# Attention scores with the low part of the keys on half of the array's rows, and an order of work without a table of corrections

## The chip, the cores and the metric

One core of one Trainium2 chip runs the whole program. The metric is the device time of one execution in microseconds (us). A run's time differs from another's of the same kernel by less than 0.2%: three runs of the kernel before took 614.14, 614.48 and 614.99 us.

## The reference, cut to what matters

Two layers, each on 256 positions of 1024 channels. One layer projects the normalised input to the operands of three causal attention mixers (a, b, c), of 8 heads of 64 channels each, and of an indexer with 8 query heads and one key head, gates each mixer's output, projects and merges the three, and adds the result to the residual.

```python
h = rms_norm(x, gain)
proj = jnp.einsum('bsd,de->bse', h, w_in)               # 9808 columns
# mixers a, b, c: per head, over the causal keys (b: over the 64 keys that the indexer picks)
s = jnp.einsum('bhqd,bhkd->bhqk', q, k) * scale         # + a forget bias in c
p = jax.nn.softmax(jnp.where(mask, s, -jnp.inf))
o = jnp.einsum('bhqk,bhkd->bhqd', p, v)
# indexer: 8 query heads, one key head
rel = jax.nn.relu(jnp.einsum('bqhd,bsd->bqhs', q_idx, k_idx))
isc = jnp.einsum('bqh,bqhs->bqs', w_idx, rel)
y = jnp.einsum('nbsw,nwd->bsnd', jnp.stack([oa, ob, oc]) , w_branch)
out = x + jnp.einsum('bsd,de->bse', jnp.sum(gates * y, axis=2), w_out)
```

## The kernel before

**Precision.** Every operand of a matmul is split into a high part (the value rounded to the type that TensorE reads in one pass) and a low part (value minus high part). A product of two operands is the sum of three products: high by high, low by high, high by low. For a weight the split is an ACT copy (`hi`, L401) and a DVE subtraction (`lo`, L405) of a 128x1024 piece; six pieces can be ready at a time (the rings `wh` and `wl`).

**Projections.** `unit_b` (L458) computes 128 output channels for all 256 positions with 24 matmuls of 256 columns, all from line 446 (`mm_ops`); `unit_a` (L475) computes 512 channels of V or of the output with matmuls of 512 columns. Three PSUM banks `proj` take turns.

**Scores.** Two heads make a pair: a projection unit gives their 64 + 64 channels on the 128 partitions. `write_q` (L611) makes three tiles: `qh`, the high part of both heads; `qx`, the high part of the first head over its low part; `qy`, the low part of the second head over its high part. `write_bd` (L766) makes the keys: `bd..h` holds two groups of 256 columns, and in group h the high part of head h stands on both halves of the partitions (one ACT copy of both heads into both groups, then one half copied across in each group, L782); `bd..l` also holds two groups of 256 columns, the low part of head 0 on the upper 64 partitions of group 0, the low part of head 1 on the lower 64 partitions of group 1, and zeros elsewhere. The zeros are written once at the start (L970 to L978). The two low parts are two DVE subtractions of 64 partitions (L784). `scores` (L626) then does, for each of two blocks of 128 queries (128 keys for the first, 256 for the second), one matmul with `qh` as the weights and both groups of `bd..l` as the moving operand (L635: 256 and 512 columns; the zeros keep the heads apart) and one matmul for each head with `qx` or `qy` as the weights and that head's `bd..h` group moving (L637: 128 or 256 columns), which adds high by high and low by high in one go, since the two stand on different rows. So bank `s0` holds the first query block of both heads, bank `s1` the second. There are 16 such groups of six matmuls in a layer (12 pairs of the mixers, 4 of the indexer), 32 in all.

**After the scores.** For a mixer's pair, DVE adds the bias and finds the extreme of each row (L696), ACT takes the exponential (L700), the normalised rows are transposed on TensorE (L723), split again (L726, L728) and multiplied with V (L739 to L742). For the indexer ACT takes the relu of the two banks (L851, L852) and DVE sums the heads (L860, L862).

**The order of the work.** The code doesn't issue instructions as it goes. It records operations, each with its engine, its cost by a formula, what it reads and writes, and a key (about the number of the projection unit to which it belongs, minus or plus a lead). `Plan.run` (L170) then places them one at a time: on the engine that can start something first, of the operations that can start then it takes the one with the lowest key. PSUM banks and buffers are handed out in that same order. What comes out is a fixed order on each engine; on the chip each engine works its list off in order and waits at semaphores. A table, `SHIFT` (L75), gives some 240 of the operations, by their number, a correction of their key (from -9 to +2).

One place in this kernel already uses a part of the array's rows: the transposes of `wf` (L798), which hold the indexer's weights and the forget logits. They read 16 partitions from partition 64 on, and the built program gives them a tile of 32 rows by 128 columns at row 64. The two matmuls at L741 and L742 use a tile of 128 rows by 64 columns at the origin. All the others use the whole array.

Of the kernel before, what the change touches and what calls it, by code (L numbers as in the profile page):

```python
# [9 lines left out]
F32 = mybir.dt.float32  # L10
# [42 lines left out]
def shape_constants():  # L53
# [18 lines left out]
    return c  # L72


SHIFT = {  # L75
# [21 lines left out]
}  # L97


CUR = [""]  # L100
PLAN_T = [0]
PREV = {}
# [19 lines left out]
class Plan:  # L122
# [8 lines left out]
    def op(self, ways, reads, writes, key, lag=0.0, name="", touch=()):  # L131
# [18 lines left out]
                o.bufs.append(t)  # L150
        o.deps = list(deps.values())
        o.n, o.out, o.need, o.end = len(self.ops), [], 0, None
        o.key += SHIFT.get(o.n, 0.0)
        for d in o.deps:
            if d is not o:
                d.out.append(o)
# [114 lines left out]
def hybrid_trunk(ctx, tc, x, norm_gain, w_in, forget_bias, w_branch, w_out, final_gain, consts, out):  # L271
# [49 lines left out]
    hTl = pool.tile([128, KC, S], F32R, name="hTl")  # L321
    og = [[pool.tile([128, 4, S], F32R, name=f"og{i}{p}") for p in "hl"] for i in range(2)]
    NBD = 3
    bd = [[pool.tile([128, 2, S], F32R, name=f"bd{i}{p}") for p in "hl"] for i in range(NBD)]
    pts = [pool.tile([128, 2, 384], F32R, name=f"pt{p}") for p in "hl"]

    cst = pool.tile([128, C_END], F32, name="cst")
# [19 lines left out]
    ncs = pool.tile([128, 2, 8], F32, name="ncs")  # L347
    widx = pool.tile([128, 2, 8], F32, name="widx")

    k_id, k_rope, k_gT, k_bdz, k_cst, k_fb, k_wf, k_widx, k_lf, k_cs = (Tok() for _ in range(10))  # L350
    k_cT, k_row = Tok(), [Tok() for _ in range(6)]
    k_isc = [Tok() for _ in range(2)]
    k_selb = [Tok() for _ in range(2)]
# [272 lines left out]
    def scores(q, k, ktoks, key, margin=MARGIN, shared=False):  # L626
        s0, s1 = Buf("s"), Buf("s")
        kt = [t for h in ktoks for t in h]
        q, kx = q

        def go():
            qh, x = T(q[0]), [T(q[1]), T(q[2])]
            kh, kl = T(k)
            for o, sl, n in ((T(s0)[:, :256], slice(0, 128), 128), (T(s1), slice(128, 256), 256)):
                PE.matmul(o.rearrange("p (h c) -> p h c", h=2), qh[:, sl], kl[:, :, :n], start=True, stop=False)  # L635
                for h in range(2):
                    PE.matmul(o[:, h * n:(h + 1) * n], x[h][:, sl], kh[:, 0 if shared else h, :n], start=False, stop=h == 1)  # L637
        pe(go, 811.0, [q[0], q[1], q[2], k] + kx + kt, [s0, s1], key, "qk", margin)
        return s0, s1

    class Pair:
# [44 lines left out]
        def attend(self, key):  # L686
# [3 lines left out]
            for h in range(2):  # L690
                b, bt, bb = bs[h]
                e, st = Buf("e"), Buf("st")
                kt = [Tok(), Tok()]
                parts = ((0, 0, 128, s0), (1, 128, 256, s1))
                for t, a, n, s in parts:
                    dve(lambda t=t, a=a, n=n, s=s, e=e, st=st, b=b, h=h: DVE.tensor_tensor_reduce(  # L696
                        T(e)[:, a:a + n], T(s)[:, h * n:(h + 1) * n], b(a, n), 1.0, 3e38, ALU.add, ALU.min,
                        T(st)[:, t:t + 1]), n, [s, bt[t]], [kt[t]], key, "max", touch=[e, st] + bb)
                for t, a, n, s in parts:
                    act(lambda t=t, a=a, n=n, e=e, st=st: ACT.activation(  # L700
# [65 lines left out]
    def write_bd(src, b, toks, key, ps, shared=False):  # L766

        up, dn = slice(0, 64), slice(64, 128)
        if not shared:
            act(lambda: ACT.activation(T(b)[0], T(src)[:, :S].unsqueeze(1).to_broadcast([128, 2, S]), AF.Copy), 2 * S, ps, [src],  # L770
                [toks[0][0], toks[0][1], toks[1][0], toks[1][1]], key, "bd", touch=[b])
        else:
            act(lambda: ACT.activation(T(b)[0][up, 0], T(src)[up, :S], AF.Copy), S, ps, [src], [toks[0][0]], key, "bd", touch=[b],
                half=True)
        for h, o in enumerate((up, dn)):
            g, x = (0, up) if shared else (h, o)
            s = lambda x=x: T(src)[x, :S]
            hi = lambda x=x, g=g: T(b)[0][x, g]
            lo = lambda o=o, h=h: T(b)[1][o, h]
            if not (shared and h):  # L780
                y = dn if x is up else up
                act(lambda hi=hi, y=y, g=g: ACT.activation(T(b)[0][y, g], hi().bitcast(F32), AF.Copy), S, False, [toks[g][0]],  # L782
                    [toks[g][1]], key, "bd", touch=[b], half=True)
            dve(lambda hi=hi, lo=lo, s=s: DVE.tensor_tensor(lo(), s(), hi().bitcast(F32), op=ALU.subtract), S,  # L784
                [src, k_bdz, toks[g][0]], [toks[h][2]], key, "bd", touch=[b], port=not ps, half=True)

    def ev_kwf(l, ps, key):
        act(lambda: ACT.activation(wf[64:80], T(ps)[64:80, :S], AF.Copy), S, True, [ps], [k_wf, k_cT], key, "wf")
# [56 lines left out]
    def index_scores(p, ps, kb, ktoks, key):  # L845
        r = rope(ps, key)
        q = write_q((lambda: T(r), r), False, key, name="qi")
        s0, s1 = scores(q, kb, ktoks, key + 1, QK_MARGIN, True)
        base = (p % 2) * 768
        rel = [tmp6[:, base:base + 256], tmp6[:, base + 256:base + 768]]  # L850
        act(lambda: ACT.activation(rel[0], T(s0)[:, :256], AF.Relu), 256, True, [s0], [k_tmp[p % 2]], key + 1, "relu")  # L851
        act(lambda: ACT.activation(rel[1], T(s1), AF.Relu), 512, True, [s1], [k_tmp[p % 2]], key + 1, "relu")  # L852
        for h in range(2):
            hd = 2 * p + h
            for t, (a, n) in enumerate(((0, 128), (128, 256))):
                rr = rel[t][:, h * n:(h + 1) * n]
                w = widx[:, t, hd:hd + 1]
                o = isc[:, a:a + n]
                if hd == 0:
                    f = lambda rr=rr, w=w, o=o: DVE.tensor_scalar(o, rr, w, None, op0=ALU.mult)  # L860
                else:
                    f = lambda rr=rr, w=w, o=o: DVE.scalar_tensor_tensor(o, rr, w, o, op0=ALU.mult, op1=ALU.add)  # L862
                dve(f, n, [k_tmp[p % 2], k_widx], [k_isc[t]], key + 1, "isc", t_dve(n) + 61.0, port=True)
# [103 lines left out]
        load(fbias.rearrange("p l h -> p (l h)"),  # L967
             forget_bias.rearrange("(o l) h -> o (l h)", o=1).to_broadcast([128, L * 8]), 8192, [k_fb], -12 + 2.6, "fb")
    late_loads()
    dve(lambda: DVE.memset(isc, 0.0), 384, [], [k_isc[0], k_isc[1]], 0.5, "zero")  # L970
    for b in bd:
        for t in b[1:]:
            z = t.rearrange("p h c -> p (h c)")
            plan.op([(e, c, lambda z=z, f=f, a=a: f(z[:, a:a + 256], isc[:, :256]))
                     for e, c, f in (("DVE", t_dve2(256), DVE.tensor_copy),) for a in (0,)],
                    [k_isc[0], k_isc[1]], [k_bdz], 1.0, 0.0, "zero")
            dve(lambda z=z: DVE.tensor_copy(z[:, 256:], isc[:, :256]), 256, [k_isc[0], k_isc[1]], [k_bdz], 1.0, "zero",
                t_dve2(256))  # L978

    hA = (lambda k, t: hTh[:, k, t * 128:(t + 1) * 128], lambda k, t: hTl[:, k, t * 128:(t + 1) * 128])  # L980
    mA = (lambda k, t: merged(k)[0][:, t * 128:(t + 1) * 128], lambda k, t: merged(k)[1][:, t * 128:(t + 1) * 128])
# [168 lines left out]
```

## Time and profile before

| what | value |
|---|---|
| median of 3 runs | 614.48 us |
| the profiled execution's own time | 614.35 us |
| its span, first to last instruction | 612.5 us |
| mean granted TensorE clock | 0.997 |
| TensorE (PE), matmuls | 4804 |
| DVE busy, of the span | 88% |
| ACT busy, of the span | 71% |
| what moved from HBM | 103.37 MB, 170 GB/s over the span |

A row of the timeline gives the start in us from the span's start, the duration in us, the engine, the line, the operation, what it writes and reads, its shapes (weights' rows*columns, then partitions x columns that move) and how many it merges. PE is a matmul and PEld the load of its weights, which the profile shows as instructions of their own. Matmuls follow one another in a pipeline: a duration of 0.28 us covers the way through the array as well, and what a matmul costs in a row of them is the distance from its start to the next one's.

### The profile page before, as it was taken

To read this page: it belongs to the slowest core of one execution; us is meant where nothing else is said; L and a number is where in the kernel's file an instruction comes from. 1 tells how busy PE (TensorE), PEld (TensorE's weight loads), DVE (VectorE), ACT (ScalarE), POOL (GpSimd) and SP (SyncE) were. 2 spreads that over 40 slices of the span, in tenths; PEclk is the share of its full clock that TensorE was granted. 3 is DMA by queue.
4 is the path that set the end of the run, shared out by engine and by line. 5 is a ranking of instruction groups with operands and counts; after the bars stand their busy time and mean duration, and the time that the engine had idled before them with its cause. 6 is when DMAs were issued, how large, how long until landed. Compare 5 with 4: busy or idle time off the path is not lost.

```text
span 612.5 us, 12615 instructions
## 1 busy us (share of the span) xinstructions
PE 603.7 (99%) x4804; PEld 580.1 (95%) x4804; DVE 536.5 (88%) x1332; ACT 437.1 (71%) x913; POOL 92.3 (15%) x98
## 2 busy tenths in 40 slices
PE   8999999999999999999999999999999999999995
PEld 6999999899998999999889999999999989999985
DVE  8899999986998899989588999999689978999873
ACT  5687597686985678875587766968689756976641
POOL 1242331000000335000006205100000014220001
PEclk9999999999999999999999999999999999999998
DMA  9963847556354655276455639284538356445411
GB/s 295 349 201 102 258 138 226 171 175 203 131 182 138 201 175 171 76 256 213 138 176 182 193 108 288 77 258 159 178 104 279 101 174 204 139 139 182 162 36 68
DMA packets 96156, 107.32 MB, mean 175 GB/s; under 512 B 4576, under 2 KB 84832, under 8 KB 96096
## 3 DMA queue, kind: packets, MB, share of 16 engines
q1 hardware_dynamic: 95808, 106.13, 54.6%
q8 instruction: 37, 0.61, 0.4%
q10 hardware_dynamic: 288, 0.39, 0.2%
q14 instruction: 23, 0.19, 0.1%
HBM read 103.37 MB, written 1.05 MB: 170 GB/s over the span
## 4 chain that ended last, share of the span: by engine, by line
PE 96%; DVE 1%; issue 1%; DMA 0%; POOL 0%; ACT 0%; POOLq 0%; DVEq 0%
PE proj L446 84%; PE t L723 3%; PE s L637 2%; PE s L635 2%; PE proj L1029 1%; PE o L742 1%; PE o L739 1%; DMA x<-in_x_dram 0%; PE o L741 0%; PE o L740 0%; DVE wl L1021 0%; DVE hTl L561 0%; DVE wh L1019 0%; PE t L547 0%; DVE tmp L513 0%
## 5 line engine op out<-in xcount | busy, mean ns | idle before, releaser
L446 PE MATMUL proj<-hTh,wh 128*128 128x256 f32 (+1 forms) x1040 | 270.3, 278 | 0.0
L446 PE MATMUL proj<-hTl,wh 128*128 128x256 f32 (+1 forms) x1040 | 270.0, 277 | 0.0
L405 DVE TENSOR_TENSOR wl<-raw,wh 128x1024 fp32r<-128x1024 f32 (+1 forms) x190 | 231.6, 1228 | 30.7 <-ACT wh L401 29.3
L446 PE MATMUL proj<-hTh,wl 128*128 128x256 f32 (+1 forms) x1040 | 234.0, 278 | 0.0
L401 ACT ACTIVATE wh<-raw 128x1024 fp32r<-128x1024 f32 (+1 forms) x190 | 199.9, 1055 | 46.9 <-PE proj L446 44.0
L446 PEld LDWEIGHTS proj<-hTh,wh 128*128 128x128 f32 (+1 forms) x1040 | 194.7, 187 | 0.3
L446 PEld LDWEIGHTS proj<-hTl,wh 128*128 128x128 f32 (+1 forms) x1040 | 194.7, 187 | 0.3
L446 PEld LDWEIGHTS proj<-hTh,wl 128*128 128x128 f32 (+1 forms) x1040 | 175.7, 187 | 0.0
L496 POOL TENSOR_TENSOR rsh<-rsh,cst 128x256 f32<-128x256 f32 (+1 forms) x42 | 35.1, 837 | 346.5 <-DVE rsh L495 346.2
L700 ACT ACTIVATE e<-e,st 128x128 f32<-128x128 f32 (+1 forms) x96 | 42.8, 449 | 12.2 <-DVE st L696 11.7
L498 POOL TENSOR_TENSOR rr<-rr,rsh 128x256 f32<-128x256 f32 (+1 forms) x42 | 50.9, 1211 | 3.6 <-DVE rr L497 0.3
L446 PE MATMUL proj<-wh,v 128*128 128x512 f32 (+1 forms) x144 | 35.5, 368 | 0.0
L446 PE MATMUL proj<-og0l,wh 128*128 128x256 f32 x128 | 33.8, 276 | 0.0
L446 PE MATMUL proj<-og0h,wh 128*128 128x256 f32 x128 | 32.3, 277 | 0.0
L446 PE MATMUL proj<-wh,hTh 128*128 128x512 f32 x80 | 32.1, 401 | 0.0
L446 PE MATMUL proj<-wh,hTl 128*128 128x512 f32 x80 | 31.3, 392 | 0.0
L446 PEld LDWEIGHTS proj<-wh,v 128*128 128x128 f32 x144 | 25.2, 188 | 4.7
L446 PE MATMUL proj<-og0h,wl 128*128 128x256 f32 x128 | 28.6, 276 | 0.0
L728 DVE TENSOR_TENSOR ptl<-t,pth 128x384 fp32r<-128x384 f32 x48 | 25.0, 550 | 1.1 <-ACT pth L726 0.9
L446 PE MATMUL proj<-wl,hTh 128*128 128x512 f32 x80 | 24.9, 392 | 0.0
L899 ACT ACTIVATE mth<-proj 128x256 f32<-128x256 f32 x32 | 12.2, 381 | 16.9 <-PE proj L446 16.8
L446 PEld LDWEIGHTS proj<-og0h,wh 128*128 128x128 f32 x128 | 24.0, 188 | 0.0
(195 smaller groups left out, 1048.4 us busy)
## 6 DMA issues: line engine op xcount, KB each, us to landing
raw<-in_w_in_dram SPq DMA_DIRECT2D x74, 1024.0 KB, 5.3
raw<-in_w_branch_dram SPq DMA_DIRECT2D x24, 512.0 KB, 3.7
raw<-in_w_out_dram SPq DMA_DIRECT2D x8, 1024.0 KB, 6.2
tmp<-wf SPq DMA_DIRECT2D x16, 128.0 KB, 5.6
raw<-in_w_in_dram SPq DMA_DIRECT2D x3, 512.0 KB, 6.6
x<-in_x_dram SPq DMA_DIRECT2D x4, 256.0 KB, 4.3
raw<-in_w_in_dram SPq DMA_DIRECT2D x2, 320.0 KB, 5.7
out_dram<-tmp SPq DMA_DIRECT2D x2, 320.0 KB, 2.4
```

The source lines that it names most:

```text
L401: ACT.activation(p[0].v, sel(c.v), AF.Copy)
L405: DVE.tensor_tensor(p[1].v, sel(c.v), p[0].v.bitcast(F32), op=ALU.subtract)
L446: PE.matmul(o(), a(), b(), start=first and i == 0, stop=last and i == n - 1)
L496: gps(lambda: POOL.tensor_tensor(T(sh)[:np_], T(sh)[:np_], s[:np_], op=ALU.mult), S, [k_rope], [sh], key, "rope")
L498: gps(lambda: POOL.tensor_tensor(T(r)[:np_], T(r)[:np_], T(sh)[:np_], op=ALU.add), S, [sh], [r], key, "rope")
L635: PE.matmul(o.rearrange("p (h c) -> p h c", h=2), qh[:, sl], kl[:, :, :n], start=True, stop=False)
L637: PE.matmul(o[:, h * n:(h + 1) * n], x[h][:, sl], kh[:, 0 if shared else h, :n], start=False, stop=h == 1)
L700: act(lambda t=t, a=a, n=n, e=e, st=st: ACT.activation(T(e)[:, a:a + n], T(e)[:, a:a + n], AF.Exp, bias=T(st)[:, t:t + 1], scale=-1.0, acc ...
L723: PE.transpose(T(ps)[:, i * 128:(i + 1) * 128], T(es[h])[:, i * 128:(i + 1) * 128], ident)
L728: dve(lambda h=h, src=src: DVE.tensor_tensor(T(pl)[:, h], src(), T(ph)[:, h].bitcast(F32), op=ALU.subtract), 384, [ps, kp[h][0]], [kp[h][1 ...
L739: PE.matmul(ov, v[:, 0, hd], T(ph)[:, h, a], start=h == 0, stop=False)
L899: act(lambda: ACT.activation(T(th), T(ps)[:, :S], AF.Tanh, scale=0.5), S, True, [ps], [th], u - EARLY, "mth")
```

## The change

- `bd..l` becomes one tile of 256 columns: the low part of head 0 on partitions 0 to 63, that of head 1 on partitions 64 to 127. There are no zeros in it, and the zeroing at the start goes. For a pair it is written by one DVE subtraction of 128 partitions, which reads group 0 of `bd..h` before head 0's high part is copied across over the lower half; that copy (ACT) now waits for the subtraction. For the indexer's single key head there are still two subtractions of 64 partitions.
- `scores` does the products with low keys as matmuls of 64 rows, one per head: head 0 with tile position (0, 0), head 1 with (64, 0). Four of them come first (both heads on 128 columns, both heads on 256), then the four with `qx` and `qy` on all 128 rows: eight matmuls for six. The moving columns are 128 + 128 + 256 + 256 in the first four, where there were 256 + 512.
- Bank `s0` now holds head 0 and bank `s1` head 1, 384 columns each. What reads the banks follows: the relu reads 384 columns of each bank where it read 256 and 512.
- The group's cost in the planner is 700 where it was 811.
- The table `SHIFT` and its use go, so that every operation's key is the one that the code gives it, and the planner's order changes on all engines.

```diff
-SHIFT = {
-    115: 1, 142: -6.5, 144: -0.5, 145: -7, 146: -1, 148: -3, 150: -5, 160: 2, 172: 2, 173: -6, 174: -1, 192: -4,
...
-        o.key += SHIFT.get(o.n, 0.0)
...
-    bd = [[pool.tile([128, 2, S], F32R, name=f"bd{i}{p}") for p in "hl"] for i in range(NBD)]
+    bd = [[pool.tile([128, 2, S], F32R, name=f"bd{i}h"), pool.tile([128, S], F32R, name=f"bd{i}l")] for i in range(NBD)]
...
-            for o, sl, n in ((T(s0)[:, :256], slice(0, 128), 128), (T(s1), slice(128, 256), 256)):
-                PE.matmul(o.rearrange("p (h c) -> p h c", h=2), qh[:, sl], kl[:, :, :n], start=True, stop=False)
+            o = [T(s0), T(s1)]
+            cols = ((slice(0, 128), 0, 128), (slice(128, 256), 128, 256))
+            for sl, a, n in cols:
                 for h in range(2):
-                    PE.matmul(o[:, h * n:(h + 1) * n], x[h][:, sl], kh[:, 0 if shared else h, :n], start=False, stop=h == 1)
-        pe(go, 811.0, [q[0], q[1], q[2], k] + kx + kt, [s0, s1], key, "qk", margin)
+                    r = slice(64 * h, 64 * h + 64)
+                    PE.matmul(o[h][:, a:a + n], qh[r, sl], kl[r, :n], start=a == 0, stop=False, tile_position=(64 * h, 0),
+                              skip_group_check=True)
+            for sl, a, n in cols:
+                for h in range(2):
+                    PE.matmul(o[h][:, a:a + n], x[h][:, sl], kh[:, 0 if shared else h, :n], start=False, stop=a > 0,
+                              skip_group_check=True)
+        pe(go, 700.0, [q[0], q[1], q[2], k] + kx + kt, [s0, s1], key, "qk", margin)
...
+        def across(y, x, g):
+            act(lambda: ACT.activation(T(b)[0][y, g], T(b)[0][x, g].bitcast(F32), AF.Copy), S, False, [toks[g][0]],
+                [toks[g][1]], key, "bd", touch=[b], half=True)
+
         if not shared:
             act(lambda: ACT.activation(T(b)[0], T(src)[:, :S].unsqueeze(1).to_broadcast([128, 2, S]), AF.Copy), 2 * S, ps, [src],
                 [toks[0][0], toks[0][1], toks[1][0], toks[1][1]], key, "bd", touch=[b])
...
+            across(up, dn, 1)
+            dve(lambda: DVE.tensor_tensor(T(b)[1], T(src)[:, :S], T(b)[0][:, 0].bitcast(F32), op=ALU.subtract), S,
+                [src, toks[0][0], toks[0][1]], [toks[0][2], toks[1][2]], key, "bd", touch=[b], port=not ps)
+            across(dn, up, 0)
+            return
...
-        act(lambda: ACT.activation(rel[0], T(s0)[:, :256], AF.Relu), 256, True, [s0], [k_tmp[p % 2]], key + 1, "relu")
-        act(lambda: ACT.activation(rel[1], T(s1), AF.Relu), 512, True, [s1], [k_tmp[p % 2]], key + 1, "relu")
+        for h, sh in enumerate((s0, s1)):
+            act(lambda h=h, sh=sh: ACT.activation(rel[h], T(sh)[:, :384], AF.Relu), 384, True, [sh], [k_tmp[p % 2]], key + 1, "relu")
...
-    dve(lambda: DVE.memset(isc, 0.0), 384, [], [k_isc[0], k_isc[1]], 0.5, "zero")
-    for b in bd:
```

PE's list, at the first group of the indexer's scores (`qh` to `qy` are the query tiles, `s` the score banks, `proj` a projection's bank), before:

```order
L446 MATMUL proj_166<-hTl,wh_67 128x256
L635 MATMUL s_167<-bd0l,qh_80 128x256
L637 MATMUL s_167<-bd0h,qx_83 128x128
L637 MATMUL s_167<-bd0h,qy_86 128x128
L635 MATMUL s_168<-bd0l,qh_80 128x512
L637 MATMUL s_168<-bd0h,qx_83 128x256
L637 MATMUL s_168<-bd0h,qy_86 128x256
L446 MATMUL proj_166<-hTh,wl_74 128x256
```

and the same place of PE's list with the change:

```order
L420 MATMUL proj_166<-hTl,wh_67 128x256
L613 MATMUL s_167<-bd0l,qh_80 128x128
L613 MATMUL s_168<-bd0l,qh_80 128x128
L613 MATMUL s_167<-bd0l,qh_80 128x256
L613 MATMUL s_168<-bd0l,qh_80 128x256
L617 MATMUL s_167<-bd0h,qx_83 128x128
L617 MATMUL s_168<-bd0h,qy_86 128x128
L617 MATMUL s_167<-bd0h,qx_83 128x256
L617 MATMUL s_168<-bd0h,qy_86 128x256
L420 MATMUL proj_166<-hTh,wl_74 128x256
```

Here nothing has moved but the group itself: the two rows with `bd0l` have become four, all ahead of the `bd0h` rows.

The third score group of mixer a in the first layer, before, on PE (it stands inside a V unit of 512-column matmuls):

```order
L446 MATMUL proj_166<-wl_74,hTh 128x512 x2
L635 MATMUL s_168<-bd0l,qh_80 128x256
L637 MATMUL s_168<-bd0h,qx_83 128x128
L637 MATMUL s_168<-bd0h,qy_86 128x128
L635 MATMUL s_167<-bd0l,qh_80 128x512
L637 MATMUL s_167<-bd0h,qx_83 128x256
L637 MATMUL s_167<-bd0h,qy_86 128x256
L446 MATMUL proj_166<-wh_68,hTh 128x512
```

and with the change (it stands inside a unit of 256-column matmuls):

```order
L420 MATMUL proj_166<-hTl,wh_67 128x256
L613 MATMUL s_167<-bd0l,qh_80 128x128
L613 MATMUL s_168<-bd0l,qh_80 128x128
L613 MATMUL s_167<-bd0l,qh_80 128x256
L613 MATMUL s_168<-bd0l,qh_80 128x256
L617 MATMUL s_167<-bd0h,qx_83 128x128
L617 MATMUL s_168<-bd0h,qy_86 128x128
L617 MATMUL s_167<-bd0h,qx_83 128x256
L617 MATMUL s_168<-bd0h,qy_86 128x256
L420 MATMUL proj_166<-hTh,wh_67 128x256
```

This group has moved up by 120 projection matmuls (756 of them stand ahead of it before, 636 now), and its fourth neighbour by 108. Of the 32 groups, 15 have moved, 10 of them up and 5 down.

More of the change, by code (lines that the diff above doesn't have):

```diff
@@ L72, in shape_constants @@
     return c
-SHIFT = {
[21 rows of a table removed]
-}
 CUR = [""]
@@ L348, in hybrid_trunk @@
     widx = pool.tile([128, 2, 8], F32, name="widx")
-    k_id, k_rope, k_gT, k_bdz, k_cst, k_fb, k_wf, k_widx, k_lf, k_cs = (Tok() for _ in range(10))
+    k_id, k_rope, k_gT, k_cst, k_fb, k_wf, k_widx, k_lf, k_cs = (Tok() for _ in range(9))
     k_cT, k_row = Tok(), [Tok() for _ in range(6)]
@@ L693, in attend @@
                 kt = [Tok(), Tok()]
-                parts = ((0, 0, 128, s0), (1, 128, 256, s1))
+                s = (s0, s1)[h]
+                parts = ((0, 0, 128, s), (1, 128, 256, s))
                 for t, a, n, s in parts:
                     dve(lambda t=t, a=a, n=n, s=s, e=e, st=st, b=b, h=h: DVE.tensor_tensor_reduce(
-                        T(e)[:, a:a + n], T(s)[:, h * n:(h + 1) * n], b(a, n), 1.0, 3e38, ALU.add, ALU.min,
+                        T(e)[:, a:a + n], T(s)[:, a:a + n], b(a, n), 1.0, 3e38, ALU.add, ALU.min,
                         T(st)[:, t:t + 1]), n, [s, bt[t]], [kt[t]], key, "max", touch=[e, st] + bb)
@@ L771, in write_bd @@
                 [toks[0][0], toks[0][1], toks[1][0], toks[1][1]], key, "bd", touch=[b])
-        else:
-            act(lambda: ACT.activation(T(b)[0][up, 0], T(src)[up, :S], AF.Copy), S, ps, [src], [toks[0][0]], key, "bd", touch=[b],
-                half=True)
-        for h, o in enumerate((up, dn)):
[L776 to L785, printed above, removed]
+            across(up, dn, 1)
[3 more added lines that the diff above has]
+            return
+        act(lambda: ACT.activation(T(b)[0][up, 0], T(src)[up, :S], AF.Copy), S, ps, [src], [toks[0][0]], key, "bd", touch=[b],
+            half=True)
+        across(dn, up, 0)
+        for h, o in enumerate((up, dn)):
+            dve(lambda o=o: DVE.tensor_tensor(T(b)[1][o], T(src)[up, :S], T(b)[0][up, 0].bitcast(F32), op=ALU.subtract), S,
+                [src, toks[0][0]], [toks[h][2]], key, "bd", touch=[b], port=not ps, half=True)
     def ev_kwf(l, ps, key):
@@ L849, in index_scores @@
         base = (p % 2) * 768
-        rel = [tmp6[:, base:base + 256], tmp6[:, base + 256:base + 768]]
-        act(lambda: ACT.activation(rel[0], T(s0)[:, :256], AF.Relu), 256, True, [s0], [k_tmp[p % 2]], key + 1, "relu")
-        act(lambda: ACT.activation(rel[1], T(s1), AF.Relu), 512, True, [s1], [k_tmp[p % 2]], key + 1, "relu")
+        rel = [tmp6[:, base + 384 * h:base + 384 * h + 384] for h in range(2)]
+        for h, sh in enumerate((s0, s1)):
+            act(lambda h=h, sh=sh: ACT.activation(rel[h], T(sh)[:, :384], AF.Relu), 384, True, [sh], [k_tmp[p % 2]], key + 1, "relu")
         for h in range(2):
@@ L855, in index_scores @@
             for t, (a, n) in enumerate(((0, 128), (128, 256))):
-                rr = rel[t][:, h * n:(h + 1) * n]
+                rr = rel[h][:, a:a + n]
                 w = widx[:, t, hd:hd + 1]
@@ L969, in hybrid_trunk @@
     late_loads()
-    dve(lambda: DVE.memset(isc, 0.0), 384, [], [k_isc[0], k_isc[1]], 0.5, "zero")
-    for b in bd:
[L972 to L978, printed above, removed]
     hA = (lambda k, t: hTh[:, k, t * 128:(t + 1) * 128], lambda k, t: hTl[:, k, t * 128:(t + 1) * 128])
```

20 rows, old and new, of the table SHIFT are left out of this document.

## Prediction

> **What bounds the kernel now.** First the page, for the load of each engine and the chain that ended last; then the whole list of what PE waited for.
>
> ```profile
> PE 603.7 (99%) x4804; PEld 580.1 (95%) x4804; DVE 536.5 (88%) x1332; ACT 437.1 (71%) x913; POOL 92.3 (15%) x98
> PE 96%; DVE 1%; issue 1%; DMA 0%; POOL 0%; ACT 0%; POOLq 0%; DVEq 0%
> PE proj L1029 <- DVE wh L1019: 1.1, 2, 0.6
> PE t L944 <- DVE ones L940: 1.1, 1, 1.1
> PE t L547 <- ACT tmp L528: 0.3, 1, 0.3
> ```
>
> TensorE is the bound, and nothing else is: it makes up 96% of the chain, and the lines of its waits (L944, L547, L1029) all lie ahead of the projections. So a change in what one score group costs TensorE arrives in the time 32 times over, unless it opens or closes a wait. The engine that could open one is DVE. Two stretches, read by window (columns: PE, PEld, DVE, ACT, POOL busy):
>
> ```profile
> 50.00:100.00 50.00, 50.00 (x442) 49.91 (x441) 49.41 (x159) 39.16 (x83) 13.39 (x14) 1.00 0.48 147
> 330.00:400.00 70.00, 70.00 (x613) 69.57 (x611) 69.30 (x196) 54.32 (x114) 21.00 (x22) 1.00 0.53 163
> ```
>
> There DVE is busy for 49.41 of 50 us and 69.30 of 70: it is level with TensorE, with nothing to spare.
>
> **The score group, step by step.** The first group of the indexer on PE, up to the projection behind it, and three of its weight loads:
>
> ```profile
> 40.88 0.28 PE L635 MATMUL s<-bd0l,qh 128*128 128x256 f32 x1
> 40.99 0.22 PE L637 MATMUL s<-bd0h,qx 128*128 128x128 f32 x1
> 41.05 0.28 PE L637 MATMUL s<-bd0h,qy 128*128 128x128 f32 x1
> 41.16 0.45 PE L635 MATMUL s<-bd0l,qh 128*128 128x512 f32 x1
> 41.45 0.28 PE L637 MATMUL s<-bd0h,qx 128*128 128x256 f32 x1
> 41.57 0.28 PE L637 MATMUL s<-bd0h,qy 128*128 128x256 f32 x1
> 41.69 0.28 PE L446 MATMUL proj<-hTh,wl 128*128 128x256 f32 x1
> 41.00 0.19 PEld L637 LDWEIGHTS s<-bd0h,qy 128*128 128x128 f32 x1
> 41.10 0.19 PEld L635 LDWEIGHTS s<-bd0l,qh 128*128 128x128 f32 x1
> 41.22 0.19 PEld L637 LDWEIGHTS s<-bd0h,qx 128*128 128x128 f32 x1
> ```
>
> The group takes 41.69 - 40.88 = 0.81 us. A matmul of 256 columns is followed 0.11 to 0.12 us later by the next. One of 128 columns could be followed sooner, but the weights of the next must be in: the loads start 0.10 and 0.12 us apart, and the matmul of 41.05 is followed only at 41.16. I count 0.11 for a load of 128 columns, hidden where it runs beside the matmul ahead.
>
> The change halves the columns that the low products stream, 768 to 384, if the two heads' halves run side by side, but it takes eight weight loads for six, and it changes the array's division twice in each group. Without a price for the second point the sum would be: the first two halves 0.11 (until the next two halves' weights are in), the next two 0.11, the four full ones 0.11 + 0.11 + 0.12 + 0.12: 0.68, so 0.13 less than now.
>
> What the switch costs can be read in one place of this trace, the transposes at L798, on a tile of 32 rows at row 64, between two ordinary matmuls (PE, then PEld):
>
> ```profile
> 25.87 0.28 PE L446 MATMUL proj<-hTh,wl 128*128 128x256 f32 x1
> 25.98 0.28 PE L446 MATMUL proj<-hTl,wh 128*128 128x256 f32 x1
> 26.19 0.29 PE L798 MATMUL t<-cst,wf 16*128 16x16 f32 x2
> 26.41 0.38 PE L446 MATMUL proj<-hTh,wh 128*128 128x256 f32 x1
> 26.63 0.28 PE L446 MATMUL proj<-hTl,wh 128*128 128x256 f32 x1
> 25.87 0.19 PEld L446 LDWEIGHTS proj<-hTl,wh 128*128 128x128 f32 x1
> 26.18 0.20 PEld L798 LDWEIGHTS t<-cst,wf 16*128 16x128 f32 x2
> 26.41 0.19 PEld L446 LDWEIGHTS proj<-hTh,wh 128*128 128x128 f32 x1
> 26.52 0.19 PEld L446 LDWEIGHTS proj<-hTl,wh 128*128 128x128 f32 x1
> ```
>
> Ahead of it the load of the next weights starts with the matmul before it (25.87 and 25.87). The small tile's load starts only at 26.18, 0.20 after its predecessor at 25.98, that is 0.09 after that one's 256 columns have gone in. Then the full load of 26.41 waits in the same way, and its matmul streams a whole load later: the next one starts at 26.63, 0.22 on instead of 0.11. From 25.98 to 26.63 pass 0.65 us, of which two full matmuls account for 0.22; 0.43 is left for two matmuls of 16 columns. So at a change of row division the next weights are not loaded ahead: about 0.09 to 0.10 us until the array is empty, and then a load of 0.11 in the open, on the way in and on the way out. A different division of the columns shows nothing of the kind:
>
> ```profile
> 97.25 0.22 PE L740 MATMUL o<-pth,v 128*128 128x128 f32 x1
> 97.31 0.22 PE L741 MATMUL o<-ptl,v 128*64 128x128 f32 x1
> 97.37 0.28 PE L742 MATMUL o<-ptl,v 128*64 128x256 f32 x1
> 97.49 0.28 PE L739 MATMUL o<-pth,v 128*128 128x256 f32 x1
> ```
>
> From a full tile to one of 64 columns and back the distances are 0.06, 0.06 and 0.12. That is the lower bound of a switch, nothing; L798 is the upper one. I take L798, since it divides the rows as the change does, though by 32 and not by 64.
>
> The Trainium skill has a rule for this: by "TensorEngine Tiling (Array Packing)", section Key Properties, changing the tiling mode drains TensorE, and changing only the tile within a mode does not. The rows at L798 agree, with 0.09 us of drain; those at L741 don't, so here the rule holds for rows at most. Against it, "TensorE: Matmul & The Clock Gate", Part 3, has matmuls of different row groups run together, about 4 ns apart; no row here shows two such tiles.
>
> Now the new group, from the moment at which it would have started before:
>
> - 0.09 until the array is empty, 0.11 for the first weights (both heads' loads side by side);
> - 0.11 for the first halves, 128 columns, until the next weights are in; 0.11 for the halves of 256 columns;
> - 0.10 until the array is empty, 0.11 for the first full weights;
> - 0.11 + 0.11 + 0.12 + 0.12 = 0.46 for the four full matmuls, by the same steps as now.
>
> That is 1.09 us for 0.81: 0.28 more, times 32 groups = 9.0 us, all of it on PE and so on the path.
>
> **The rest of the change.** Rows for it: the low parts on DVE, DVE's weight splits, ACT's waits for a free weight buffer, DVE's first wait, and the score groups by stage (two L635 matmuls each).
>
> ```profile
> L784 DVE TENSOR_TENSOR bd1l<-rr,bd1h x14: 410/423/950, 77.4 to 555.0; 64x256 fp32r<-64x256 f32 x14
> L405 DVE TENSOR_TENSOR wl<-raw,wh 128x1024 fp32r<-128x1024 f32 (+1 forms) x190 | 231.6, 1228 | 30.7 <-ACT wh L401 29.3
> ACT wh L401 <- PE proj L446: 44.0, 48, 1.9
> 3.70 0.69 DVE L513 CUSTOM_DVE_ANT_0 tmp<-x 128x512 f32<-128x512 f32 x1 [0.95 <-DMA x<-in_x_dram]
> 0.00:50.00 50.00, 2.90 (x8) 1.51 (x8) 1.00 0.89 287
> 50.00:100.00 50.00, 1.45 (x4) 0.76 (x4) 1.00 0.48 147
> ```
>
> *Low parts of the keys.* One subtraction for two in 24 pairs: 24 x 0.42 = 10 us less of DVE, which is not on the path: nothing now, a reserve against the next point. *Zeros at the start.* DVE waits 0.95 us for x at 3.70 with them done; nothing. *The new wait.* ACT's copy across waits for the subtraction, at most about 0.42 us, and behind it on ACT queue the weight copies, for which DVE's splits wait. ACT is 71% busy and itself waited 44.0 us for PE to free weight buffers; nothing, or 0.42 for a pair where that lead is gone. *Relu.* 384 + 384 columns for 256 + 512; nothing. *SP.* Some loads of the forget rows change place with weight loads; nothing, while the rings are full.
>
> *The table.* Without it the order of all engines differs, and score groups stand up to 120 matmuls earlier. Nothing in the trace of before shows its worth: PE has no wait between the first projections and the end, so it can't gain. The lower bound is nothing. For the upper, DVE is full at 50 to 100 and 330 to 400 us, and a weight split that is put one operation too late there costs PE up to its 1.23 us; at two such places in each layer, 4 x 1.23 = 4.9 us. With the switches I take nothing: by 100 us PE has done six groups (8 + 4 matmuls at L635) and runs 6 x 0.28 = 1.7 us later, DVE gaining that much time. Without them PE would be 6 x 0.13 = 0.8 us early, and I take one split, 1.2.
>
> **Sum.** The profiled execution took 614.35 us, 1.85 outside its span and 0.13 below the median; 614.35 + 9.0 = 623.3.
>
> **Rivals.**
>
> 1. *Faster: no drain for halves.* If a 64-row tile's weights load ahead as the 64-column tile's do at L741, the group is 0.68: 32 x 0.13 = 4.2 us less, 610.2, and with one split late 611.4 (610.2 to 615.1 by the bounds of the table). For it speaks L741; against it L798, where both switches show the delay. It decides below a cost of 0.13 us for both switches of a group.
> 2. *Drain, and no overlap.* The two heads' loads go one after the other through the one load path that the rows show at 0.11 each. Then 0.09, five steps of 0.11 (four loads and the last stream), 0.10, 0.11 and 0.46: 1.31, 0.50 more, 16.0 in all: 630.4. For it: no two loads in the rows above start closer than 0.10. Against it: all of those load the same rows.
> 3. *The change doesn't do what it says: neither drain nor overlap.* Four halves at 0.11 each, and 0.46: 0.90, so 32 x 0.09 = 2.9: 617.2.
> 4. *Drain, and the order starves PE as well*, by the 4.9 above: 628.2. For it: DVE is full twice; against it: the later PE.
>
> **How the numbers follow.** Forecast 0.48 (its own range 620 to 627, for 0.05 us less at each emptying or a second load half hidden); rival 1 0.26; rival 2 0.14; rival 3 0.06; rival 4 0.06. The range, 610 to 627.5, holds the forecast, rivals 1 and 3, and leaves out 2 and 4, 0.20 together. A measurement of this kernel tells 0.2%, 1.2 us, from no change. Rival 1 gives faster 0.23 and, with most of its bound for the table used up, same 0.03; the others are slower, 0.74.
>
> **What would show it.** In the trace after: the first low-key load of a group starting 0.2 us after the full matmul ahead of it, not beside it; two halves starting within a few hundredths of each other; the distance from the first half to the projection behind the group 0.9 us, and about 1.1 with the gap ahead of it; PE still without waits for DVE. Loads that start beside the matmul ahead, with a group of 0.68, mean rival 1. Halves 0.11 apart mean rival 2 or 3. Waits of PE for `wl`, or gaps between projections away from the groups, mean that the table was worth its place, and I would have its price wrong.

## The result and the profile after

The changed kernel takes 622.5 us (median of four, 622.27 to 622.66) where the kernel before takes 614.49: a ratio of 1.013, interval 1.0118 to 1.0143. Slower by 8.0 us; 623.3 was forecast, by the case that was thought likeliest. The profiled execution took 622.27 us, with a span of 620.5. One of the later runs of the kernel before, beside the experiments, took 670.61 us at a granted clock of 0.85 (0.997 to 0.999 in all the others); it is in none of the ratios.

The page's load of the engines, its chain, and the list of all of PE's waits, in the changed kernel:

```profile
PE 611.5 (99%) x4868; PEld 581.4 (94%) x4868; DVE 522.8 (84%) x1286; ACT 441.5 (71%) x924; POOL 92.4 (15%) x102
PE 96%; DVE 1%; issue 1%; DMA 0%; POOL 0%; ACT 0%; POOLq 0%; DVEq 0%
PE proj L1004 <- DVE wh L994: 1.2, 2, 0.6
PE t L928 <- DVE half L925: 1.1, 1, 1.1
PE t L521 <- ACT tmp L502: 0.4, 1, 0.4
```

TensorE is busy 611.5 us for 603.7, and its waits still all lie in the first 13 us. DVE has 13.7 us less to do. So the 8 us are TensorE's own work, and no other engine put them there. The first score group of the indexer shows where they arise (PE, then PEld; "x4" merges the four halves):

```profile
40.42 0.28 PE L420 MATMUL proj<-hTh,wh 128*128 128x256 f32 x1
40.53 0.28 PE L420 MATMUL proj<-hTl,wh 128*128 128x256 f32 x1
40.73 0.50 PE L613 MATMUL s<-bd0l,qh 64*128 64x128 f32 x4
41.16 0.33 PE L617 MATMUL s<-bd0h,qx 128*128 128x128 f32 x1
41.33 0.28 PE L617 MATMUL s<-bd0h,qy 128*128 128x128 f32 x1
41.44 0.33 PE L617 MATMUL s<-bd0h,qx 128*128 128x256 f32 x1
41.61 0.28 PE L617 MATMUL s<-bd0h,qy 128*128 128x256 f32 x1
41.72 0.28 PE L420 MATMUL proj<-hTh,wl 128*128 128x256 f32 x1
40.08 0.30 PEld L420 LDWEIGHTS proj<-hTh,wl 128*128 128x128 f32 x2
40.42 0.19 PEld L420 LDWEIGHTS proj<-hTl,wh 128*128 128x128 f32 x1
40.73 0.30 PEld L613 LDWEIGHTS s<-bd0l,qh 64*128 64x128 f32 x4
41.16 0.19 PEld L617 LDWEIGHTS s<-bd0h,qx 128*128 128x128 f32 x1
41.27 0.19 PEld L617 LDWEIGHTS s<-bd0h,qy 128*128 128x128 f32 x1
```

Between ordinary matmuls a load starts with the matmul ahead of it (40.42 and 40.42). The first halves' load starts 0.20 us after the matmul of 40.53, and the first full load behind the halves at 41.16, where the four halves started at 40.73: no load runs ahead over either change of division. The four loads of the halves all lie within 0.30 us, as much as two loads that follow one another take elsewhere (40.08). One by one, without the merging, the trace has the two heads' first loads at 40.734 and 40.737 and their matmuls at 40.735 and 40.739: the two halves run side by side. From 40.53 to 41.72 it is 1.19 us; take off the 0.11 of the matmul at 40.53, and the group costs 1.08, where it cost 0.81. (The row of a half starts with its load here, 40.73 for both. So the distance from the first half to the projection is 0.99 us, and not the 0.9 that the prediction gave as a sign.) Worked out over all 32 groups, from the start of the matmul ahead to the start of the one behind, it is 38.23 us for 30.14: 8.1 more. All other distances on PE together, from the first projection on, are 568.4 us for 568.3.

### The profile page after: what moved, and what is told of

The parts are those of the page before. It is cut to its first block, busy times and chain, and to the rows that moved or that the text cites. A ratio compares the mean times of both kernels' runs of the same rounds, so it can differ in the third digit from the quotient of the medians.

```text
span 620.5 us, 12685 instructions
## 1 busy us (share of the span) xinstructions
PE 611.5 (99%) x4868; PEld 581.4 (94%) x4868; DVE 522.8 (84%) x1286; ACT 441.5 (71%) x924; POOL 92.4 (15%) x102
## 4 chain that ended last, share of the span: by engine, by line
PE 96%; DVE 1%; issue 1%; DMA 0%; POOL 0%; ACT 0%; POOLq 0%; DVEq 0%
PE proj L420 83%; PE s L617 3%; PE t L705 3%; PE s L613 2%; PE proj L1004 1%; PE o L724 1%; PE o L721 1%; PE o L723 0%; PE o L722 0%; DMA x<-in_x_dram 0%; DVE wl L996 0%; DVE hTl L535 0%; DVE wh L994 0%; PE t L521 0%; PE s L521 0%
## 5 line engine op out<-in xcount | busy, mean ns | idle before, releaser
L379 DVE TENSOR_TENSOR wl<-raw,wh 128x1024 fp32r<-128x1024 f32 (+1 forms) x190 | 234.4, 1238 | 42.2 <-ACT wh L375 41.4
L470 POOL TENSOR_TENSOR rsh<-rsh,cst 128x256 f32<-128x256 f32 (+1 forms) x42 | 31.3, 744 | 390.6 <-DVE rsh L469 390.5
L682 ACT ACTIVATE e<-e,st 128x128 f32<-128x128 f32 x96 | 42.5, 445 | 4.8 <-DVE st L678 4.6
L737 ACT ACTIVATE ot<-o 64x256 f32<-64x256 f32 x48 | 18.3, 381 | 10.6 <-PE o L724 9.6
L420 PE MATMUL proj<-wl,hTh 128*128 128x512 f32 x80 | 24.9, 391 | 0.0
```

Source lines behind the costliest of these rows:

```text
L379: DVE.tensor_tensor(p[1].v, sel(c.v), p[0].v.bitcast(F32), op=ALU.subtract)
L420: PE.matmul(o(), a(), b(), start=first and i == 0, stop=last and i == n - 1)
L470: gps(lambda: POOL.tensor_tensor(T(sh)[:np_], T(sh)[:np_], s[:np_], op=ALU.mult), S, [k_rope], [sh], key, "rope")
L682: act(lambda t=t, a=a, n=n, e=e, st=st: ACT.activation(T(e)[:, a:a + n], T(e)[:, a:a + n], AF.Exp, bias=T(st)[:, t:t + 1], scale=-1.0, acc ...
L737: act(lambda r=r, h=h: ACT.activation(T(t)[r], T(o)[64:, h * S:(h + 1) * S], AF.Copy), S, True, [o], [kt[h]], key, "og", touch=[t], half=True)
```

## The experiments

All medians are of runs next to runs of the kernel before on the same chip (614.4 to 614.6 us).

**The table alone.** The kernel before, with an empty table.

```diff
-SHIFT = {
-    115: 1, 142: -6.5, 144: -0.5, 145: -7, 146: -1, 148: -3, 150: -5, 160: 2, 172: 2, 173: -6, 174: -1, 192: -4,
...
-}
+SHIFT = {}
```

> The kernel before with an empty table and nothing else changed. Theory (the table is worth nothing here, the 8 us are the score groups): 614.5 us, within 1.2; PE has no waits between the first projections and the end, and its score groups take 0.81 us as before. Rival (part of the 8 us is starvation that the table prevented): up to 4 x 1.23 = 4.9 us slower, 616 to 619.4, with gaps of PE in front of projections in the stretches in which DVE is full.

Measured: 616.75 us, ratio 1.0035, interval 1.0021 to 1.0049. The theory is wrong: it isn't nothing. By its time the rival is right, near the low end of its 616 to 619.4; but the gaps don't stand where it put them, in the stretches in which DVE is full. The largest of them, on PE and then on DVE:

```profile
237.14 0.39 PE L424 MATMUL proj<-og1h,wl 128*128 128x256 f32 x2
237.93 0.39 PE L424 MATMUL proj<-hTh,wh 128*128 128x256 f32 x1 [0.41 <-DVE rr L475]
236.31 0.56 DVE L706 TENSOR_TENSOR ptl<-t,pth 128x384 fp32r<-128x384 f32 x1 [0.86 <-ACT pth L704]
237.13 0.45 DVE L473 STREAM_SHUFFLE rsh<-proj 128x256 f32<-128x256 f32 x1
237.47 0.41 DVE L475 TENSOR_TENSOR rr<-proj,cst 128x256 f32<-128x256 f32 x1
```

PE wants a `proj` bank that DVE has not finished reading for the rotary embedding. DVE is late there because it was itself released late: up to 236.31 it stood idle for 0.86 us, waiting for ACT, and from there on it works without a pause. The same gap stands in the second layer. From matmul to matmul the two come to 1.1 us, half of what the missing table costs; smaller ones, up to 0.4 us, stand at score groups, transposes and the products with V. So the table has a worth in the kernel before, 2.3 us, and none of these gaps is a wait for a weight split, as I had priced it.

**Without the division.** The changed kernel, its low-key products on all 128 rows against keys with zeros; the data's layout and its two subtractions are those of before.

```diff
...
-                    r = slice(64 * h, 64 * h + 64)
-                    PE.matmul(o[h][:, a:a + n], qh[r, sl], kl[r, :n], start=a == 0, stop=False, tile_position=(64 * h, 0),
-                              skip_group_check=True)
+                    PE.matmul(o[h][:, a:a + n], qh[:, sl], kl[:, h, :n], start=a == 0, stop=False, skip_group_check=True)
...
```

> The changed kernel with its low-key products on all 128 rows, against keys with zeros as before: still eight matmuls per group, four of them ahead, a bank per head, no table; only the division of the array into halves is gone. Theory (the two switches per group cost): four low products at 0.11 us each and 0.46 for the others, 0.90 a group, 0.09 more than before: 32 x 0.09 = 2.9 over 614.5, 617.4 us, and weight loads that start beside the matmul ahead of them. Rival (it is the two more loads, the banks or the order of the eight): 622.5 us as the changed kernel.

Measured: 618.92 us, ratio 1.0072, interval 1.0056 to 1.0087. The group, PE and PEld:

```profile
40.80 0.28 PE L420 MATMUL proj<-hTl,wh 128*128 128x256 f32 x1
40.91 0.62 PE L612 MATMUL s<-bd0l,qh 128*128 128x128 f32 x4
41.82 0.28 PE L420 MATMUL proj<-hTh,wl 128*128 128x256 f32 x1
40.80 0.53 PEld L612 LDWEIGHTS s<-bd0l,qh 128*128 128x128 f32 x4
41.26 0.19 PEld L615 LDWEIGHTS s<-bd0h,qx 128*128 128x128 f32 x1
```

The same eight matmuls without a division: the load starts with the matmul ahead (40.80), and the group costs 41.82 - 40.91 = 0.91 us, as expected. The eight matmuls for six and their order explain 0.10 of the 0.27 us; the rest is the division. The time is 1.5 us above the 617.4 expected. Of gaps, 1.1 us stand away from the groups (the other distances sum to 569.5 us for 568.4) and 0.6 at one score group that waits for DVE. Most of the 1.1 us is the gap of the run with the empty table, the wait for the rotary embedding once in each layer.

**Twice as many switches.** The changed kernel, each block's halves right ahead of its own full matmuls: a loop header and nothing else.

```diff
             for sl, a, n in cols:
                 for h in range(2):
                     r = slice(64 * h, 64 * h + 64)
                     PE.matmul(o[h][:, a:a + n], qh[r, sl], kl[r, :n], start=a == 0, stop=False, tile_position=(64 * h, 0),
                               skip_group_check=True)
-            for sl, a, n in cols:
                 for h in range(2):
```

> The changed kernel with each query block's halves right ahead of its own two full matmuls, so that the array's division changes four times in a group and not twice; the same eight matmuls. Theory (each change of division costs about 0.10 us of emptying and 0.11 of an open load, while two matmuls of 128 columns then cost 0.06 and not 0.11): 2 x 0.21 - 0.10 = 0.32 more a group, 32 x 0.32 = 10.2 us over 622.5, 632.7. Rival (the cost hangs on the halves themselves or comes once a group): 622.5, within 1.5.

Measured: 631.6 us, ratio to before 1.0278, interval 1.0264 to 1.0292; 9.1 above the changed kernel, 10.2 expected. PE, then PEld:

```profile
41.09 0.28 PE L420 MATMUL proj<-hTl,wh 128*128 128x256 f32 x1
41.29 0.33 PE L613 MATMUL s<-bd0l,qh 64*128 64x128 f32 x2
41.29 0.19 PEld L613 LDWEIGHTS s<-bd0l,qh 64*128 64x128 f32 x2
41.55 0.19 PEld L616 LDWEIGHTS s<-bd0h,qx 128*128 128x128 f32 x1
41.92 0.19 PEld L613 LDWEIGHTS s<-bd0l,qh 64*128 64x128 f32 x2
42.23 0.19 PEld L616 LDWEIGHTS s<-bd0h,qx 128*128 128x128 f32 x1
```

The rows are the first load behind each of the four changes, and each is held back: by 0.20 us after the matmul of 41.09, and the others, at 41.55, 41.92 and 42.23, until the matmuls between have gone through. The group costs 1.37 us, 0.29 more than with two switches, and 32 x 0.29 = 9.3. With the 0.10 that the expectation allowed for cheaper matmuls of 128 columns, two more switches cost 0.39, that is 0.20 each: the price is one per switch.

**The one division that before had.** The kernel before, with the transposes of `wf` over the whole array.

```diff
...
-                PE.transpose(T(ps)[:, t * 16:t * 16 + 16], wf[64:80, t * 128:(t + 1) * 128], ident[64:80, 64:80])
+                PE.transpose(T(ps)[:, t * 128:(t + 1) * 128], wf[:, t * 128:(t + 1) * 128], ident)
...
```

> The kernel before, with the transposes of wf (L798) over all 128 partitions instead of 16 on a tile of 32 rows; the rest of wf is set to zero once at the start. Theory (the gap there is a change of row division): the 0.65 us from the full matmul ahead to the second one behind become about 0.45 (four steps of 0.11), 0.2 less in each of two layers: 614.1 us, less than a time can tell, so the distances decide. Rival (PE waits there for ACT's copy of wf): the load still starts 0.20 us after the matmul ahead, and the time is 614.5.

Measured: 614.01 us, ratio 0.9993, interval 0.9984 to 1.0002: not told apart by its time from the 614.43 of the kernel before. The distances decide (PE):

```profile
26.26 0.28 PE L446 MATMUL proj<-hTl,wh 128*128 128x256 f32 x1
26.37 0.38 PE L798 MATMUL t<-cst,wf 128*128 128x128 f32 x2
26.51 0.36 PE L446 MATMUL proj<-hTh,wh 128*128 128x256 f32 x1
26.71 0.28 PE L446 MATMUL proj<-hTl,wh 128*128 128x256 f32 x1
```

The 0.65 us are 0.45, by moving eight times as many columns through eight times as many rows. The gap was not a wait for ACT, whose copy of `wf`, 0.38 us from 24.9 on, was done 0.9 us before the load of 26.18 in the kernel before.

**All halves.** The changed kernel with the other products on 64-row tiles too; the copies that stacked high and low parts go.

```diff
...
+            prods = ((qh, kl), (ql, kh), (qh, kh))
+            for i, (x, y) in enumerate(prods):
+                for sl, a, n in cols:
+                    for h in range(2):
+                        r = slice(64 * h, 64 * h + 64)
+                        PE.matmul(o[h][:, a:a + n], x[r, sl], y[r, :n], start=i == 0 and a == 0, stop=i == 2 and a > 0,
+                                  tile_position=(64 * h, 0), skip_group_check=True)
...
```

> The changed kernel with all products of a score group on 64-row tiles: three products (low keys, low queries, high by high) on two query blocks, each as two halves side by side; qx, qy's copies and the copies across of the keys go. Twelve matmuls in six pairs, one way in and one way out. Theory (two tiles load and stream at once, so a pair costs one step of 0.11; the switches are the rest): 0.20 + 6 x 0.11 + 0.20 = 1.06 a group for 1.08, 621.9 us, though TensorE has half as many matmuls again in a group. Rival (two halves side by side still take a step each): six steps of 0.11 more, 32 x 0.64 = 21 over 622.5, 643.

Measured: 623.68 us, ratio to before 1.015, interval 1.0132 to 1.0168. PE, and the load behind the group:

```profile
40.67 0.28 PE L420 MATMUL proj<-hTl,wh 128*128 128x256 f32 x1
40.88 0.50 PE L607 MATMUL s<-bd0l,qh 64*128 64x128 f32 x4
41.22 0.40 PE L607 MATMUL s<-bd0h,qy 64*128 64x128 f32 x4
41.45 0.39 PE L607 MATMUL s<-bd0h,qh 64*128 64x128 f32 x4
41.77 0.19 PEld L420 LDWEIGHTS proj<-hTh,wl 128*128 128x128 f32 x1
```

Twelve matmuls with two switches cost what eight do, within 0.02 us: from the load at 40.88 to the load at 41.77 it is 0.89; less the first load (0.11) and the delay of the load behind the last columns (0.09, as in the changed kernel), 0.69 for six pairs, 0.115 a pair. Two halves load and stream in one step. The 0.6 us that I had expected to gain is a loss of 1.2, half of it in the group (0.115 a step for 0.11, 1.10 in all).

**The planner's cost.** The changed kernel with `pe(go, 1080.0, ...)` for `pe(go, 700.0, ...)`.

> The changed kernel with the planner's cost of a score group at 1080 and not 700, so that the order is planned for what the group takes; the instructions are the same. Theory (PE has no waits in the changed kernel that an order could take away): 622.5 us, within 1.2. Rival (the wrong cost of 700 put things in a bad order, and some of the 8 us is that): 620 or less.

Measured: 623.92 us, ratio to before 1.0154, interval 1.0138 to 1.017. Not better but 1.4 worse: with another order one score group comes 0.6 us later, waiting for DVE, and smaller gaps make up the rest. So planning for the right cost doesn't bring any of the 8 us back.

**One tile, nothing else.** The changed kernel, its low-key matmuls over all rows of the same operands; all other engines keep their instructions and their order. Nothing keeps the low products of the two heads apart here.

```diff
-                    r = slice(64 * h, 64 * h + 64)
-                    PE.matmul(o[h][:, a:a + n], qh[r, sl], kl[r, :n], start=a == 0, stop=False, tile_position=(64 * h, 0),
-                              skip_group_check=True)
+                    PE.matmul(o[h][:, a:a + n], qh[:, sl], kl[:, :n], start=a == 0, stop=False, skip_group_check=True)
```

> The changed kernel with its four low-key matmuls on all 128 rows of the same operands, and not a row of any other engine changed (each head's scores then also hold the other head's low-key product). The group costs what it does in the run with full rows, 0.91 for 1.08: 32 x 0.17 = 5.5 less than 622.5, 617.0, if PE finds no new waits. Theory (the changed kernel needs no table because the switches make PE late, and the waits come back when they go): 1 to 2 us of gaps on PE, 618 to 619. Rival (it is the lighter DVE, 24 subtractions fewer, that stands in for the table): no gaps, 617.0.

Measured: 617.38 us, ratio to before 1.0047, interval 1.0031 to 1.0063. This is the change's two parts laid apart: 2.9 us for eight matmuls instead of six, 5.1 for the division. The 1 to 2 us of gaps that the theory asked for don't come: without the table and without the switches the other distances on PE sum to 568.2 us, for 568.4 in the changed kernel. One gap is left, at one of the 32 score groups (PE; the first group of the indexer, then that one):

```profile
40.90 0.62 PE L612 MATMUL s<-bd0l,qh 128*128 128x128 f32 x4
41.35 0.22 PE L615 MATMUL s<-bd0h,qx 128*128 128x128 f32 x1
379.91 0.92 PE L612 MATMUL s<-bd0l,qh 128*128 128x128 f32 x4
380.67 0.22 PE L615 MATMUL s<-bd0h,qx 128*128 128x128 f32 x1
```

The four low-key matmuls take 0.76 us at 379.91 where they take 0.45 at 40.90: the second head's matmul waits for its score bank, which DVE still reads (L676). In the changed kernel the same group is 0.04 us longer than the others. So PE, late by its switches, covers 0.3 us and no more. The time agrees with the rival's 617.0 and this gap, but the run doesn't show that it is the lighter DVE which keeps PE fed: the order without the table is planned for other work than in the run with the empty table.

**The subtraction twice,** in that run and in the changed kernel: the same DVE instruction, a second time in its place.

```diff
-            dve(lambda: DVE.tensor_tensor(T(b)[1], T(src)[:, :S], T(b)[0][:, 0].bitcast(F32), op=ALU.subtract), S,
-                [src, toks[0][0], toks[0][1]], [toks[0][2], toks[1][2]], key, "bd", touch=[b], port=not ps)
+            dve(lambda: [DVE.tensor_tensor(T(b)[1], T(src)[:, :S], T(b)[0][:, 0].bitcast(F32), op=ALU.subtract)
+                         for _ in range(2)], S, [src, toks[0][0], toks[0][1]], [toks[0][2], toks[1][2]], key, "bd", touch=[b], port=not ps)
```

> The run with one tile (low-key matmuls on all rows, 617.4 us), with the subtraction that writes a pair's low keys done twice in its place: 24 DVE instructions of about 0.42 us more, 10 us, as many as before; no order changes on any engine. Theory (the lighter DVE stood in for the table): gaps on PE come back, 1 to 2 us, 618.4 to 619.4. Rival (the order planned for the changed kernel is good by itself, whatever DVE carries): 617.4, within 0.6.

> The changed kernel with the same subtraction done twice, 10 us more of DVE, the same order. Theory of the prediction (PE, late by its switches, leaves DVE the time): no gaps, 622.5 us, within 0.6. Rival (lateness of PE doesn't help, since what DVE does is released by PE): gaps as in the run with one tile and the doubled subtraction, 623.5 to 624.5.

Measured: 620.91 us for the run with one tile (1.0101, interval 1.0085 to 1.0118), 625.1 for the changed kernel (1.0171, interval 1.0156 to 1.0186). So 3.5 us more without switches and 2.6 more with them, and both are above what either side had expected (619.4 and 624.5 at most). PE in the stretch from 330 to 400 us, in the run with one tile and with the subtraction twice in it; then two of its matmuls:

```profile
330.00:400.00 70.00, 69.91 (x619) 69.77 (x618) 68.64 (x196) 54.59 (x114) 20.84 (x23) 1.00 0.56 174
```

```profile
330.00:400.00 70.00, 69.38 (x612) 69.04 (x611) 67.98 (x198) 53.55 (x112) 21.28 (x24) 1.00 0.54 165
382.87 0.33 PE L612 MATMUL s<-bd0l,qh 128*128 128x128 f32 x1 [0.39 <-DVE st L676]
383.42 0.61 PE L612 MATMUL s<-bd0l,qh 128*128 128x128 f32 x3 [0.23 <-DVE st L676]
```

Here the score group waits for the banks of the one before, which DVE still reads (L676). With the order kept, 10 us more on DVE bring gaps back in both kernels; a PE that is late by its switches hides about 0.9 of 3.5 us, no more than the intervals leave open. The doubled instruction also stands right ahead of the scores, so these runs don't part DVE's load from the path to a group; that stays open. And the gaps are others than those of the missing table: PE waits for the rotary embedding's reading of a bank 0.8 us with the empty table and 0.6 in the run without the division, which both write the keys as before, and not at all in the changed kernel, the run with one tile and the two with the subtraction twice. So without a table these waits go with the old writing of the keys and the order planned for it, and not with DVE's load alone.

## Why the prediction was right, and where not

- *TensorE is the bound, and a group's cost arrives 32 times.* Right: 8.1 us in the groups, 0.1 elsewhere, 8.0 in the time.
- *The switch, taken from L798.* Right, though that place divides by 32 rows: 0.20 us to the load there and here. Doubling the switches and taking L798's own away both gave the price again, 0.29 for 0.32 and 0.20 for 0.20. The lower bound, from the tiles of 64 columns at L741, doesn't hold for rows.
- *Overlap of the two heads.* Right: four loads in 0.30 us, and 0.115 a pair in the run of all halves. Rivals 2 and 3 fall with it, rival 1 with the loads held back, and rival 4 with a PE that has no new waits.
- *The sum, 9.0.* Too high by 1.0, in two parts. Between matmuls of 256 columns a group costs 0.27 us more and not 0.28, 8.6 in all. And before, four of the 32 distances start at a matmul of 512 columns, which takes 0.12 us longer, so that the sum over the groups grows by 8.1 alone. The second part is only a matter of where a distance starts: those matmuls are still there in the changed kernel, among the others, whose sum should have grown by 0.5 and grew by 0.1. What shortened them by the rest, no run shows.
- *The table at nothing.* The number was right, its reason mostly was not, so this was in part luck. I let the late PE cover for the missing table. The run with one tile has no late PE, and its only gap is 0.3 us: so much the lateness covers. The rest this change doesn't need: the order planned for its own work, with 24 subtractions fewer, keeps PE fed, and which of the two does it, the order or the lighter DVE, stays open. In the kernel before the table is worth 2.3 us, inside the bound of 4.9, but for another cause than weight splits. No run shows rival 1's 1.2 us for one split.
- *Zeros, relu, ACT's new wait, SP.* Nothing each, as said: PE has no wait for any of them.

## What to carry to other kernels

Halving the rows of a matmul to run two side by side halves the columns that TensorE has to stream for them. But each change from the whole array to row tiles and back held the next weight load back and left it in the open, here for 0.20 us each way. So it pays only where a run of tiled matmuls saves more than both, and a score group of four halves saved 0.13 by the prediction's sum. Here the price could be read ahead of time, from the one place where the kernel already used a few rows. And where TensorE has no gaps, count its weight loads too: eight matmuls for six cost 0.10 us a group, some 3 us in all.

## What the runs showed of the hardware that was not expected

- A transpose of 16 rows on a row tile is slower, between ordinary matmuls, than the same transposes over 128 rows: 0.65 us for 0.45 from the full matmul ahead to the second behind.
- A change in the division of columns (128 to 64 and back, L741) doesn't hold the next load back; a change in the division of rows does, by the same 0.20 us for tiles of 32 rows and of 64. The Trainium skill, "TensorEngine Tiling (Array Packing)", section Key Properties, has one rule for both; here the rows bear it out and the columns don't.
- One DVE instruction of about 0.42 us, added 24 times to a kernel whose TensorE had one gap of 0.3 us, cost 3.5 us of its 10.
